# Bilinear form on one Trainium2 core: casting weight transfers of 1 MiB to 128 partitions, with a block diagonal x over four k

## The chip, the cores and the metric

The kernel runs on one core of one Trainium2 chip, with nothing on the others. The metric is the device time of one execution in microseconds (us). The kernel before was run three times.

TensorE (PE in the profile) multiplies into PSUM, with its weight loads shown apart as PEld; VectorE (DVE) does elementwise work and reductions; GpSimd (POOL) issues the transfers that change the type of what they move; SyncE (SP) and ScalarE (ACT) issue plain transfers.

## The reference

```python
def setup_inputs():
    batch, dim_i, dim_j, dim_k = 32, 256, 256, 128
    # x [32, 256], y [32, 256], weight [128, 256, 256], all float32

def reference(x, y, weight):
    return np.einsum('bi,bj,kij->bk', x, y, weight).astype(np.float32)
```

For each batch row b and each k, out[b, k] is x[b] times the 256 x 256 matrix weight[k] times y[b]. The weights are 33.55 MB in float32, and each of them is used once. Both kernels first form x[b] times weight[k] on TensorE, a row of 256 values over j, and then multiply that row by y[b] and sum over j on VectorE.

## The kernel before, in words

The weights come in by transfers from GpSimd's queue, which read float32 in HBM and write bf16 in SBUF, so 16.78 MB are written. There are 32 steps (the loop over kt), each for four k. A step's buffer, wtile, has 128 partitions in two halves of 64, and two k in each half (even k in the lower half, odd k in the upper). Each half is filled by a transfer of its own (L82): 64 partitions, two k, and per partition and k four rows of i side by side, a run of 4 KiB in HBM and of 2 KiB in SBUF. That makes 64 transfers with 128 runs each, 512 KiB read and 256 KiB written apiece. Four buffers turn (wpool, bufs=4), so the ninth transfer and each second one after it wait until TensorE has finished with the buffer of four steps ago.

TensorE makes 16 products per step (L95). Partition ip of a half holds the rows 4·ip to 4·ip+3 of i, so the sum over i takes four products (ic = 0 to 3) of 64 partitions each; the stationary operand is a 64 x 32 piece of xT, and the moving one is 64 x 256 weights of one k. Products for the lower and the upper half of the partitions alternate. The result for one k is a PSUM tile of 32 x 256, and four such tiles turn (psum, bufs=4).

VectorE takes each of these 128 results (L113): it multiplies 32 x 256 values by y and sums along j in one instruction, and a short second one writes the sum into a column of out_sb. At the end SP writes out_sb, 32 rows of 512 B (L124).

Ahead of this, x is loaded twice side by side (L53, L54), y once (L58), GpSimd makes a 32 x 32 identity (in masks.py, with the first weight transfer issued between its two steps), and TensorE transposes x in four pieces (L66), which VectorE copies to bf16 (L71).

Of the kernel before, what the change touches and what calls it, by code (L numbers as in the profile page):

```python
# [1 line left out]

# [5 lines left out]


@with_exitstack
def kernel(
    ctx: ExitStack,
    tc: tile.TileContext,
    x: bass.AP,
    y: bass.AP,
    weight: bass.AP,
    out: bass.AP,
):
    nc = tc.nc  # L20
    P = 128

    B, I = x.shape
    _, J = y.shape
    K, _, _ = weight.shape
    assert x.shape == (B, I)
    assert y.shape == (B, J)
    assert weight.shape == (K, I, J)
    assert out.shape == (B, K)

    CHUNK = 4
    HALF_P = P // 2
    assert I == HALF_P * CHUNK
    assert K <= P
    assert K % 2 == 0

    K_TILE = 4
    assert K % K_TILE == 0 and K_TILE % 2 == 0
    K_HALF = K_TILE // 2
    NUM_K_TILES = K // K_TILE  # L40
    K_SUB = max(1, min(K_HALF, 256 // J))
    assert K_HALF % K_SUB == 0

    f32 = mybir.dt.float32
    bf16 = mybir.dt.bfloat16

    consts = ctx.enter_context(tc.tile_pool(name="consts", bufs=1))
    wpool = ctx.enter_context(tc.tile_pool(name="wpool", bufs=4))
    psum_pool = ctx.enter_context(tc.tile_pool(name="psum", bufs=4, space=bass.MemoryType.PSUM))
    tmps = ctx.enter_context(tc.tile_pool(name="tmps", bufs=2))  # L50

    x2_sb = consts.tile([B, 2, I], f32)
    nc.sync.dma_start(out=x2_sb[:, 0, :], in_=x)  # L53
    nc.sync.dma_start(out=x2_sb[:, 1, :], in_=x)  # L54
    x2_flat = x2_sb.rearrange("b two i -> b (two i)")

    y_sb = consts.tile([B, J], f32)
    nc.sync.dma_start(out=y_sb, in_=y)  # L58

    identB = consts.tile([B, B], f32)  # L60
    make_identity(nc, identB)

    xT = consts.tile([P, CHUNK, B], bf16)
    for ic in range(CHUNK):
        xt_psum = psum_pool.tile([P, B], f32)
        nc.tensor.transpose(  # L66
            out=xt_psum,
            in_=x2_flat[:, ic::CHUNK],
            identity=identB,
        )  # L70
        nc.vector.tensor_copy(out=xT[:, ic, :], in_=xt_psum)  # L71

    out_sb = consts.tile([B, K], f32)

    w_rearr = weight.rearrange("k (ip ic) j -> ip k (ic j)", ic=CHUNK)

    for kt in range(NUM_K_TILES):
        k0 = kt * K_TILE

        wtile = wpool.tile([P, K_HALF, CHUNK * J], bf16)  # L80
        for kg in range(2):
            nc.gpsimd.dma_start(  # L82
                out=wtile[kg * HALF_P:(kg + 1) * HALF_P, :, :],
                in_=w_rearr[:, k0 + kg:k0 + K_TILE:2, :],
            )

        for ks in range(0, K_HALF, K_SUB):
            psums = []
            for kg in range(2):
                psum = psum_pool.tile([P, K_SUB * J], f32)  # L90
                psums.append(psum)
            for ic in range(CHUNK):
                for kg in range(2):
                    p0 = kg * HALF_P
                    nc.tensor.matmul(  # L95
                        out=psums[kg][:B, :].rearrange(
                            "b (k j) -> b k j", k=K_SUB
                        ),
                        lhsT=xT[p0:p0 + HALF_P, ic, :],
                        rhs=wtile[p0:p0 + HALF_P, ks:ks + K_SUB,  # L100
                                  ic * J:(ic + 1) * J],
                        start=(ic == 0),
                        stop=(ic == CHUNK - 1),
                    )

            for kg in range(2):
                psum_view = psums[kg][:B, :].rearrange(
                    "b (k j) -> b k j", k=K_SUB
                )
                for kk in range(K_SUB):  # L110
                    kdst = k0 + 2 * (ks + kk) + kg
                    tmp = tmps.tile([B, J], f32)
                    nc.vector.tensor_tensor_reduce(  # L113
                        out=tmp,
                        in0=psum_view[:, kk, :],
                        in1=y_sb,
                        scale=1.0,
                        scalar=0.0,
                        op0=mybir.AluOpType.mult,
                        op1=mybir.AluOpType.add,  # L120
                        accum_out=out_sb[:, kdst:kdst + 1],
                    )

    nc.sync.dma_start(out=out, in_=out_sb)  # L124


# [1 line left out]
_INS = ['x', 'y', 'weight']  # L128
_OUTS = [((32, 128), 'float32')]


# [23 lines left out]
```

## Time and profile before

| what | value |
|---|---|
| median of 3 runs | 92.71 us (92.67 to 92.99) |
| span of the profiled execution, first to last instruction | 90.9 us |
| median less span (what lies around the span) | 1.8 us |
| written by the weight queue (q0) | 16.78 MB in 9216 packets |
| HBM read | 33.65 MB |
| busy: PE, DVE, POOL | 73.9, 49.8, 38.0 us |

The profiled execution's own end-to-end time isn't given apart from its span; it is taken here as the span and the 1.8 us that the median has beyond it.

How to read it: the span is what the profiler saw between the first and the last instruction. In the table of stretches (windows), each row names a stretch in us from the span's start, its length, then the busy time of each engine in it with the number of instructions started, the granted clock of TensorE, the share in which the 16 DMA engines had a packet (it can exceed 1, since packets overlap), and the rate in GB/s, counted in bytes written. Since the weights are written in bf16, the rate of reading them is twice that. In the table of instruction groups, each row has the line, the engine, the operation, the tiles, the shape, the count, the busy time, the mean of one in ns, and the idle time of the engine ahead of them with what ended it.

### The profile page before, as it was taken

The page shows a single profiled execution, that of the slowest core. Times are in us where ns is not written, and L with a number is a line of the kernel's source. Part 1 is how long each engine was busy: PE and PEld are TensorE (multiplying, and loading weights), DVE is VectorE, ACT ScalarE, POOL GpSimd, SP SyncE. Part 2 cuts the span into 40 slices and gives each one's busy share as a digit, 9 for nine tenths or more (in the row PEclk, how much of TensorE's full clock was granted, in tenths as well). Part 3 has the DMA queues.
Part 4 walks back from the last instruction along what each step waited for, and adds up shares of the span by engine and source line. Part 5 has one row for each costly group of instructions (what it writes and reads, how often), then busy time and mean ns, then how long its engine had stood idle before and what let it go on. Part 6 is the DMA issues. An engine that isn't in the chain of part 4 may idle for free.

```text
span 90.9 us, 1569 instructions
## 1 busy us (share of the span) xinstructions
PE 73.9 (81%) x516; PEld 42.3 (47%) x516; DVE 49.8 (55%) x260; POOL 38.0 (42%) x70
## 2 busy tenths in 40 slices
PE   0248989899898989669898989898998989899970
PEld 0216444555454545435554545454555545454530
DVE  0213555676535666664556656666555565566650
POOL 5970555544435543650455554434345555500000
PEclk9999999999999999985555555555555555555555
DMA  0799999999999999999999999999999999999300
GB/s 18 121 190 186 197 208 210 207 211 213 207 208 210 208 210 209 209 209 209 211 208 212 209 209 209 211 208 215 203 210 208 211 208 212 207 210 214 53 0 7
DMA packets 9416, 16.99 MB, mean 187 GB/s; under 512 B 1088, under 2 KB 1216, under 8 KB 9408
## 3 DMA queue, kind: packets, MB, share of 16 engines
q0 software_dynamic: 9216, 16.78, 100.1%
q1 hardware_dynamic: 192, 0.11, 0.5%
q8 instruction: 4, 0.07, 0.3%
q14 instruction: 4, 0.03, 0.1%
HBM read 33.65 MB, written 0.02 MB: 370 GB/s over the span
## 4 chain that ended last, share of the span: by engine, by line
DMA 64%; PE 20%; POOL 6%; issue 6%; DVE 1%; DVEq 0%; POOLq 0%
DMA wtile<-in_weight_dram 64%; PE psum L95 20%; POOL wtile L82 6%; DVE tmp L113 1%; DVE out_sb L113 0%; POOL identB masks.py:199 0%; DVEq L150 0%; POOL identB masks.py:197 0%; POOLq masks.py:199 0%; POOLq L139 0%
## 5 line engine op out<-in xcount | busy, mean ns | idle before, releaser
L95 PE MATMUL psum<-wtile,xT 64*32 64x256 bf16 x512 | 73.2, 405 | 11.1 <-DMA wtile<-in_weight_dram 9.3
L113 DVE CUSTOM_DVE_ANT_0 tmp<-psum,y_sb 32x256 f32<-32x256 f32 x128 | 48.6, 409 | 35.4 <-PE psum L95 35.2
L95 PEld LDWEIGHTS <-xT 64*32 64x32 bf16 x512 | 41.8, 122 | 42.2 <-DMA wtile<-in_weight_dram 23.9
L82 POOL DMA_DIRECT2D wtile<-in_weight_dram x64 | 37.5, 596 | 40.7 <-PE psum L95 40.1
L113 DVE DVE_READ_ACCUMULATOR2_ANT out_sb<- 32x1 f32 x128 | 9.1, 71 | 0.0
L66 PE MATMUL xt_psum<-identB,x_sb 32*128 32x32 f32 x4 | 0.7, 300 | 3.0 <-DMA x_sb<-in_x_dram 3.0
L71 DVE CAST xT<-xt_psum 128x32 bf16<-128x32 f32 x4 | 0.6, 192 | 3.4 <-PE xt_psum L66 3.4
L66 PEld LDWEIGHTS xt_psum<-identB,x_sb 32*128 32x128 f32 x4 | 0.6, 208 | 3.0 <-POOL identB masks.py:199 3.0
masks.py:199 POOL TENSOR_SCALAR_AFFINE_SELECT identB<-identB 32x32 f32<-32x32 f32 x1 | 0.2, 229 | 0.1
masks.py:197 POOL MEMSET identB<- 32x32 f32 x1 | 0.1, 114 | 0.3 <-POOLq L139 0.3
L139 POOL MEMSET const-float32-0.0<- 128x1 f32 x1 | 0.1, 103 | 0.2 <-issue 0.2
L139 POOL MEMSET const-bfloat16-1.0<- 128x1 bf16 x1 | 0.1, 106 | 0.0
L139 POOL MEMSET const-uint8-127<- 128x1 uint8 x1 | 0.1, 106 | 0.0
L139 POOL MEMSET const-float32-1.0<- 128x1 f32 x1 | 0.1, 103 | 0.0
## 6 DMA issues: line engine op xcount, KB each, us to landing
wtile<-in_weight_dram POOLq DMA_DIRECT2D x64, 256.0 KB, 7.2
x_sb<-in_x_dram SPq DMA_DIRECT2D x2, 32.0 KB, 1.7
y_sb<-in_y_dram SPq DMA_DIRECT2D x1, 32.0 KB, 3.2
out_dram<-out_sb SPq DMA_DIRECT2D x1, 16.0 KB, 1.4
```

Source lines behind the costliest of these rows:

```text
L66: nc.tensor.transpose(out=xt_psum, in_=x2_flat[:, ic::CHUNK], identity=identB,)
L71: nc.vector.tensor_copy(out=xT[:, ic, :], in_=xt_psum)
L82: nc.gpsimd.dma_start(out=wtile[kg * HALF_P:(kg + 1) * HALF_P, :, :], in_=w_rearr[:, k0 + kg:k0 + K_TILE:2, :],)
L95: nc.tensor.matmul(out=psums[kg][:B, :].rearrange("b (k j) -> b k j", k=K_SUB), lhsT=xT[p0:p0 + HALF_P, ic, :], rhs=wtile[p0:p0 + HALF_P, ...
L113: nc.vector.tensor_tensor_reduce(out=tmp, in0=psum_view[:, kk, :], in1=y_sb, scale=1.0, scalar=0.0, op0=mybir.AluOpType.mult, op1=mybir.Al ...
L139: nc = _bacc.Bacc("TRN2", target_bir_lowering=False, num_devices=1)
```

## The change

All transfers now fill 128 partitions. The index k is split as k = 32·kk + g with kk from 0 to 3 and g from 0 to 31, and i as i = 8·ip + ic with ip from 0 to 31 and ic from 0 to 7. Partition p = 4·ip + kk holds, for one g, the eight rows ic of i for the k that belongs to kk: one run of 8 KiB in HBM and of 4 KiB in SBUF. Neighbouring partitions with the same ip are 32 k apart in HBM, which is 8 MiB. One transfer fills a step (1 MiB read, 512 KiB written, 128 runs), except the last step, which is cut into three (ic 0 to 3, 4 and 5, 6 and 7). There are 34 transfers, each with a buffer of its own, so all weights stay in SBUF as bf16 and no transfer waits for a buffer.

The stationary operand becomes block diagonal: xblk[p, ic, b, kk'] is x[b, 8·ip + ic] where kk' is the kk of the partition p, and zero elsewhere. One product of 128 partitions by 128 columns by 256 then serves 32 rows of the batch and four k at once, and its result has 128 rows (b, kk). Eight products (ic) make a step: 256 in all, in place of 512. VectorE reduces one 128 x 256 result per step, 32 in place of 128, and the output goes out as 128 rows of 128 B.

The setup changes with it: x is loaded once, y is loaded on ACT's queue to 128 partitions with each row repeated four times, the identity is 128 x 128, VectorE repeats x four times (8 copies) and makes a mask from the identity (one reduction), TensorE transposes in eight pieces, and VectorE writes xblk with four masked copies.

The diff, cut to its core (the body of the old loop and the old setup are in the listing above):

```diff
+    w_v = weight.rearrange("(kk g) (ip ic) j -> g ip kk (ic j)", kk=KK, ic=IC)
+    x_sb = consts.tile([B, I], f32)
+    nc.sync.dma_start(out=x_sb, in_=x)
+    y4 = consts.tile([P, J], f32)
+    nc.scalar.dma_start(out=y4, in_=y.unsqueeze(1).to_broadcast([B, KK, J]))
+
+    def split(g):
+        return [(0, 4), (4, 6), (6, 8)] if g == G - 1 else [(0, IC)]
+
+    def load(g):
+        for lo, hi in split(g):
+            wt = wpool.tile([P, (hi - lo) * J], bf16, name=f"w{g}_{lo}")
+            nc.gpsimd.dma_start(out=wt, in_=w_v[g][:, :, lo * J:hi * J])
...
+    load(0)
+    ident = consts.tile([P, P], f32)
+    nc.gpsimd.memset(ident, 0.0)
+    nc.gpsimd.affine_select(
...
+    for g in range(1, G):
+        load(g)
+    mask = consts.tile([P, KK], f32)
+    nc.vector.tensor_reduce(
...
+    for ic in range(IC):
+        nc.vector.tensor_copy(
+            out=x_rep[:, ic, :, :],
+            in_=x_cols[:, ic, :].unsqueeze(2).to_broadcast([B, IP, KK]),
+        )
+    xt_ps = psx.tile([P, IC, B], f32)
+    for ic in range(IC):
         nc.tensor.transpose(
...
+    xblk = consts.tile([P, IC, B, KK], bf16)
+    for kk in range(KK):
+        nc.vector.tensor_scalar(
+            out=xblk[:, :, :, kk], in0=xt_ps, scalar1=mask[:, kk:kk + 1],
+            scalar2=None, op0=mult,
+        )
...
+    for g in range(G):
+        ps = pso.tile([P, J], f32)
+        for ic in range(IC):
+            nc.tensor.matmul(
+                out=ps,
+                lhsT=xblk[:, ic, :, :].rearrange("p b kk -> p (b kk)"),
+                rhs=w_tiles[g, ic],
+                start=(ic == 0), stop=(ic == IC - 1),
+            )
+        tmp = tmps.tile([P, J], f32)
+        nc.vector.tensor_tensor_reduce(
+            out=tmp, in0=ps, in1=y4, scale=1.0, scalar=0.0,
+            op0=mult, op1=add, accum_out=acc[:, g:g + 1],
+        )
+    out_v = out.rearrange("b (kk g) -> b kk g", kk=KK)
+    nc.sync.dma_start(out=out_v, in_=acc)
```

How the instructions stand is shown for two places. The first is GpSimd's queue at the beginning of the kernel before, from the barrier that opens the program (wtile is a weight buffer, in_weight_dram the weights in HBM; the sizes are partitions, runs in a partition and elements of a run; DMASW names the completion count of an earlier weight transfer, PE that of a product).

```order
L150 UNCONDITIONAL_BRANCH [waits barrier_Pool_Activation_PE_DVE_SP_gather]
masks.py:197 MEMSET identB 32x32
L82 DMA wtile<-in_weight_dram 64x2x1024
masks.py:199 ISA
masks.py:199 AFFINE_SELECT identB<-identB 32x32 [waits Pool_49]
L82 DMA wtile<-in_weight_dram 64x2x1024 x7
L82 DMA wtile<-in_weight_dram 64x2x1024 [waits DMASW1_49,DMASW0_49,PE_49]
```

The same place in the changed kernel (w_0 stands for the weight buffers, which now have names of their own).

```order
L144 UNCONDITIONAL_BRANCH [waits barrier_Pool_Activation_PE_DVE_SP_gather]
L56 DMA w_0_74<-in_weight_dram 128x1x2048
L63 MEMSET ident 128x128
L56 DMA w_0_81<-in_weight_dram 128x1x2048
L64 ISA
L64 AFFINE_SELECT ident<-ident 128x128 [waits Pool_49]
L56 DMA w_0_83<-in_weight_dram 128x1x2048
...
L56 DMA w_0_95<-in_weight_dram 128x1x2048 [waits DMASW0_49]
```

The first weight transfer now stands ahead of the identity's memset, a second one stands ahead of the identity's last step, and the ninth transfer (w_0_95) waits for the completion of the first alone, no longer for TensorE.

The second place is TensorE's queue at the end of the kernel before: the products of the last step, with their waits for VectorE to free a PSUM tile.

```order
L95 MATMUL psum<-wtile,xT 32x256 [waits DVE_49]
L95 LDWEIGHTS xT
L95 MATMUL psum<-wtile,xT 32x256 [waits DVE_49]
L95 LDWEIGHTS xT
L95 MATMUL psum<-wtile,xT 32x256
```

The same place in the changed kernel: the last step's three pieces (w_0_141 has four products, the other two have two each).

```order
L105 LDWEIGHTS xblk [waits DMASW7_49]
L105 MATMUL ps<-w_0_141,xblk 128x256 [waits DVE_49]
...
L105 LDWEIGHTS xblk
L105 MATMUL ps<-w_4_143,xblk 128x256 [waits DMASW0_49]
...
L105 LDWEIGHTS xblk
L105 MATMUL ps<-w_6_145,xblk 128x256 [waits DMASW1_49]
L105 LDWEIGHTS xblk
L105 MATMUL ps<-w_6_145,xblk 128x256
L144 UNCONDITIONAL_BRANCH
```

What stood behind a step's last transfer were its sixteen products and four reductions; now two products stand behind the wait for the last piece, and one reduction behind those.

More of the change, by code (lines that the diff above doesn't have):

```diff
@@ L7 @@
 from concourse._compat import with_exitstack
-from concourse.masks import make_identity
 @with_exitstack
@@ L21 @@
     P = 128
+    f32 = mybir.dt.float32
+    bf16 = mybir.dt.bfloat16
+    mult = mybir.AluOpType.mult
+    add = mybir.AluOpType.add
     B, I = x.shape
@@ L25 @@
     K, _, _ = weight.shape
[L26 to L45, printed above, removed]
+    KK = P // B
@@ L47 @@
+    IP = P // KK
+    IC = I // IP
+    G = K // KK
+    assert KK * B == P and IP * KK == P and IC * IP == I and G * KK == K
     consts = ctx.enter_context(tc.tile_pool(name="consts", bufs=1))
-    wpool = ctx.enter_context(tc.tile_pool(name="wpool", bufs=4))
-    psum_pool = ctx.enter_context(tc.tile_pool(name="psum", bufs=4, space=bass.MemoryType.PSUM))
+    wpool = ctx.enter_context(tc.tile_pool(name="wpool", bufs=1))
+    psx = ctx.enter_context(tc.tile_pool(name="psx", bufs=1, space=bass.MemoryType.PSUM))
@@ L50 @@
+    pso = ctx.enter_context(tc.tile_pool(name="pso", bufs=6, space=bass.MemoryType.PSUM))
     tmps = ctx.enter_context(tc.tile_pool(name="tmps", bufs=2))
[L52 to L63, printed above, removed]
@@ L64 @@
-    for ic in range(CHUNK):
-        xt_psum = psum_pool.tile([P, B], f32)
+    w_v = weight.rearrange("(kk g) (ip ic) j -> g ip kk (ic j)", kk=KK, ic=IC)
[5 more added lines that the diff above has]
+        return [(0, 4), (4, 6), (6, 8)] if g == G - 1 else [(0, IC)]
+    w_tiles = {}
+    def load(g):
+        for lo, hi in split(g):
+            wt = wpool.tile([P, (hi - lo) * J], bf16, name=f"w{g}_{lo}")
+            nc.gpsimd.dma_start(out=wt, in_=w_v[g][:, :, lo * J:hi * J])
+            for ic in range(lo, hi):
+                w_tiles[g, ic] = wt[:, (ic - lo) * J:(ic - lo + 1) * J]
@@ new lines @@
+    load(0)
+    ident = consts.tile([P, P], f32)
+    nc.gpsimd.memset(ident, 0.0)
+    nc.gpsimd.affine_select(
+        out=ident, in_=ident, compare_op=mybir.AluOpType.not_equal, fill=1.0,
+        base=0, pattern=[[-1, P]], channel_multiplier=1,
+    )
[3 more added lines that the diff above has]
+    nc.vector.tensor_reduce(
+        out=mask, in_=ident.rearrange("p (ip kk) -> p kk ip", kk=KK),
+        axis=mybir.AxisListType.X, op=add,
+    )
+    x_rep = consts.tile([B, IC, IP, KK], f32)
@@ L66 @@
+    x_cols = x_sb.rearrange("b (ip ic) -> b ic ip", ic=IC)
+    for ic in range(IC):
[5 more added lines that the diff above has]
+    for ic in range(IC):
         nc.tensor.transpose(
-            out=xt_psum,
-            in_=x2_flat[:, ic::CHUNK],
-            identity=identB,
-        )
-        nc.vector.tensor_copy(out=xT[:, ic, :], in_=xt_psum)
@@ L73 @@
[L73 to L84, printed above, removed]
-            )
[L87 to L122, printed above, removed]
@@ L124 @@
-    nc.sync.dma_start(out=out, in_=out_sb)
+            out=xt_ps[:, ic, :],
+            in_=x_rep[:, ic, :, :].rearrange("b ip kk -> b (ip kk)"),
+            identity=ident[:B, :B],
+        )
+    xblk = consts.tile([P, IC, B, KK], bf16)
[4 more added lines that the diff above has]
+        )
+    acc = consts.tile([P, G], f32)
+    for g in range(G):
[6 more added lines that the diff above has]
+                start=(ic == 0), stop=(ic == IC - 1),
+            )
+        tmp = tmps.tile([P, J], f32)
+        nc.vector.tensor_tensor_reduce(
+            out=tmp, in0=ps, in1=y4, scale=1.0, scalar=0.0,
+            op0=mult, op1=add, accum_out=acc[:, g:g + 1],
+        )
```

## The prediction

> **What bounds the kernel now.** I read the page first: the slices, the queues, the chain that ended last.
>
> ```profile
> span 90.9 us, 1569 instructions
> DMA  0799999999999999999999999999999999999300
> DMA packets 9416, 16.99 MB, mean 187 GB/s; under 512 B 1088, under 2 KB 1216, under 8 KB 9408
> q0 software_dynamic: 9216, 16.78, 100.1%
> DMA 64%; PE 20%; POOL 6%; issue 6%; DVE 1%; DVEq 0%; POOLq 0%
> ```
>
> The DMA engines are busy from the second slice to the third from last, and the chain leads through them for 64% of the span. PE is busy for 81% of it, so I looked at what it waits for, in the groups by line.
>
> ```profile
> L95 PE MATMUL psum<-wtile,xT 64*32 64x256 bf16 x512 | 73.2, 405 | 11.1 <-DMA wtile<-in_weight_dram 9.3
> L113 DVE CUSTOM_DVE_ANT_0 tmp<-psum,y_sb 32x256 f32<-32x256 f32 x128 | 48.6, 409 | 35.4 <-PE psum L95 35.2
> L113 DVE DVE_READ_ACCUMULATOR2_ANT out_sb<- 32x1 f32 x128 | 9.1, 71 | 0.0
> L82 POOL DMA_DIRECT2D wtile<-in_weight_dram x64 | 37.5, 596 | 40.7 <-PE psum L95 40.1
> ```
>
> TensorE waits for weights, VectorE for TensorE, and GpSimd for TensorE to free a buffer. GpSimd's 40.1 us of waiting would matter if the queue ran empty. The stretches say that it doesn't (stretch, length, then PE, PEld, DVE, POOL, the clock, the DMA share, GB/s written):
>
> ```profile
> 1.00:10.00 9.00, 4.29 (x27) 2.55 (x29) 2.54 (x14) 5.67 (x11) 1.00 0.88 148
> 10.00:84.00 74.00, 65.81 (x468) 37.74 (x466) 44.53 (x234) 32.00 (x55) 0.70 1.12 210
> 84.00:86.00 2.00, 1.89 (x15) 1.04 (x11) 1.10 (x5) 0.00 (x0) 0.50 0.40 71
> ```
>
> For 74 us the rate is 210 GB/s written, 420 read. Together: 9 x 148 + 74 x 210 + 2 x 71 = 17,014 KB, the page's 16.99 MB. So the time is a start, a stream at 210, and a tail. The start and the end of the stream:
>
> ```profile
> 3.20:3.40 0.20, 0.20 (x4) 0.20 (x3) 0.03 (x1) 0.20 (x1) 1.00 0.17 20
> 3.40:3.60 0.20, 0.20 (x3) 0.16 (x2) 0.20 (x2) 0.20 (x2) 1.00 0.93 113
> 3.60:3.80 0.20, 0.09 (x1) 0.10 (x1) 0.20 (x3) 0.20 (x1) 1.00 0.87 184
> 5.00:10.00 5.00, 3.64 (x23) 1.91 (x24) 1.99 (x10) 2.03 (x5) 1.00 1.11 185
> 85.40:85.60 0.20, 0.20 (x4) 0.01 (x1) 0.20 (x1) 0.00 (x0) 0.50 0.17 31
> 85.60:85.80 0.20, 0.20 (x2) 0.00 (x0) 0.20 (x3) 0.00 (x0) 0.50 0.01 0
> ```
>
> Weights flow from about 3.4 us, at the full rate after a ramp that loses 0.2. From 5 to 10 us the rate is 185, which costs 5 x 25 / 210 = 0.6 us, for a reason that I don't see. About 0.13 MB other than weights (instructions above all; 0.21 MB less what moved before 3.4) take 0.5. So 3.4 + 0.2 + 16.78 MB / 210 (79.9) + 0.6 + 0.5 = 84.6, where the stream would end at the full rate; since the engines finish apart, the last data come at 85.6, 0.9 to 1.0 later.
>
> **The change part by part.** *The stream.* The same 16.78 MB are written, and the rate decides. The queue's 9216 packets are 64 x 144: on each of 16 engines a transfer is 8 data packets and one more small one (1024 of the page's 1088 under 512 B). A transfer takes 262 KB / 210 = 1.248 us. After, 8 data packets carry twice the bytes. Lower bound of a gain: if time goes by bytes alone, 210 stays. Upper bound: if each of the 9 packets costs a fixed 1.248 / 9 = 139 ns for its present size, and only the small packet's share is halved, 512 KiB take 8 x 277 + 139 = 2.36 us, 222 GB/s. The share of 1.12 says that packets overlap on an engine and hide much of what is fixed, so I stay near the low end: 213.5, that is 78.6 us, 1.3 less than now.
>
> The Trainium skill, "DMA: Bandwidth & Descriptors", section "Bandwidth", prices a packet's fixed overhead at about 3 cycles of 32 B; by that, an estimate, 4 KiB reads cost 131 cycles and 8 KiB reads 259, a gain of 1.2% or some 0.9 us (the rate would be 212.5), and its ceiling of 435 GB/s read is 217.6 written, 77.1 us. No row before the change separates the fixed part from the bytes.
>
> *The start.* GpSimd issues the first weight transfer ahead of the memset, not behind it.
>
> ```profile
> 0.74 0.11 POOL masks.py:197 MEMSET identB<- 32x32 f32 x1 [0.29 <-POOLq L139]
> 1.28 0.72 POOL L82 DMA_DIRECT2D wtile<-in_weight_dram  x1 [0.42 <-issue]
> 2.24 4.10 POOL L82 DMA_DIRECT2D wtile<-in_weight_dram  x7
> ```
>
> The memset's 0.11 us is the gain; data come 2.1 us after the issue (1.28 to 3.4), so from 3.3. Each issue takes 0.6 us of GpSimd for the same 128 runs but now feeds 2.45 us of transfers, so the second one may stand behind a memset, and the ramp of 0.2 us shrinks to 0.1. Of the dips of 0.6 us I keep 0.3 (bounds 0 and 0.6). Other data: 0.4 in place of 0.5, with half of TensorE's instructions to fetch. The larger y moves while the first weights are being issued.
>
> *Setup behind that.* x lands 1.7 us after its issue and its first transfer suffices. Eight copies, eight transposes in their cover, a reduction and four masked copies follow. Nearest rows: the old casts and transposes, and L113 for 256 elements on VectorE.
>
> ```profile
> L66 PE MATMUL xt_psum<-identB,x_sb 32*128 32x32 f32 x4 | 0.7, 300 | 3.0 <-DMA x_sb<-in_x_dram 3.0
> L71 DVE CAST xT<-xt_psum 128x32 bf16<-128x32 f32 x4 | 0.6, 192 | 3.4 <-PE xt_psum L66 3.4
> x_sb<-in_x_dram SPq DMA_DIRECT2D x2, 32.0 KB, 1.7
> ```
>
> 8 x 0.19 + 0.41 + 0.3 + 4 x 0.41 = 3.9 us from about 2.5, so xblk stands at 6.4 (at 0.41 for each copy too, 8.1). The first step lands at about 3.3 + 2.45 + 0.4 = 6.2. At worst TensorE starts 1.9 us late, with 75 us to catch up, and no transfer waits for it any more. Cost nothing; the stream covers it.
>
> *The products.* A step now brings eight of 128 partitions and 128 columns, in 2.45 us: 306 ns for each.
>
> ```profile
> 40.92 2.29 PE L95 MATMUL psum<-wtile,xT 64*32 64x256 bf16 x16 [0.60 <-DMA wtile<-in_weight_dram]
> 38.48 1.04 PE L95 MATMUL psum<-wtile,xT 64*32 64x256 bf16 x12 [0.71 <-DVE out_sb L113]
> L95 PE MATMUL psum<-wtile,xT 64*32 64x256 bf16 x22 | 2.4, 271 | 0.9 <-DVE out_sb L113 0.7 <-DMA wtile<-in_weight_dram 0.2
> L95 PE MATMUL psum<-wtile,xT 64*32 64x256 bf16 x98 | 14.7, 411 | 2.0 <-DMA wtile<-in_weight_dram 1.7 <-DVE out_sb L113 0.2
> L95 PE MATMUL psum<-wtile,xT 64*32 64x256 bf16 x102 | 14.7, 412 | 1.4 <-DMA wtile<-in_weight_dram 1.4
> L95 PEld LDWEIGHTS <-xT 64*32 64x32 bf16 x512 | 41.8, 122 | 42.2 <-DMA wtile<-in_weight_dram 23.9
> ```
>
> The rows with x22, x98 and x102 are the groups of three stretches: 37.3 to 40.2, 20 to 36, and 60 to 76 us. Sixteen take 2.29 us with the last one's 0.41: (2.29 - 0.41) / 15 = 125 ns apart, and since two halves of the partitions alternate, 250 ns within a half. That is the row for a product of 256 columns. Shorter is possible: the twelve at 38.48, of 0.27 each, stand (1.04 - 0.27) / 11 = 70 apart, 140 within a half. Longer: if all of the 122 ns of a weight load came on top, 372. I take 250, 2.0 us per step, and TensorE waits for the stream. VectorE has 32 x 0.48 us in place of 128.
>
> *The tail.* Before, the last step shows this:
>
> ```profile
> 83.61 1.69 PE psum L95 x8
> 86.10 1.69 PE psum L95 x8
> 88.57 0.01 DVE out_sb L113
> 88.61 0.33 SPq L124 DMA_DIRECT2D out_dram<-out_sb  x1
> out_dram<-out_sb SPq DMA_DIRECT2D x1, 16.0 KB, 1.4
> y_sb<-in_y_dram SPq DMA_DIRECT2D x1, 32.0 KB, 3.2
> ```
>
> From 86.10 it takes 2.48 us to VectorE's end at 88.58, and 2.3 from there to the end of the span, 4.8 in all. After: two products (0.25 + 0.41), one reduction with its short second part (0.03 + 0.41 + 0.07), 1.2 us; then 2.3, and for 128 rows of 128 B in place of 32 of 512 B I add 0.2 (bounds: 0, and 1.5, since y landed in 3.2 us where x took 1.7). 3.7 in all.
>
> *The sum.* 3.3 + 0.1 + 78.6 + 0.3 + 0.4 = 82.7; 0.9 for engines that finish apart, 83.6; 0.4 from the last data to the first product, 84.0 (before: 85.6 to 86.1, partly the queue of results); tail 3.7: a span of 87.7 in place of 90.9. With the 1.8 us that the median has beyond the span: 89.5 us.
>
> **The rivals.** *The rate stays at 210.* Time goes by bytes, or a run of 8 KiB is moved as two. The stream takes 79.9, the time is 90.8. For it: 210 hardly moves over 74 us. Against it: the small packets that go. The change would then not do to the rate what its larger runs stand for.
>
> *The rate rises to the upper bound.* At 217 to 222 GB/s the stream takes 77.3 to 75.6, and the time is 88.2 to 86.5. Single rows of 1 us reach that, none lasts:
>
> ```profile
> 22.00:23.00 1.00, 0.77 (x9) 0.43 (x9) 0.70 (x6) 0.94 (x2) 1.00 1.12 219
> 23.00:24.00 1.00, 1.00 (x8) 0.58 (x5) 0.42 (x2) 0.23 (x1) 1.00 1.12 203
> ```
>
> *Slower: reads that lie 8 MiB apart disturb each other.* Before, a transfer reads two k that are 512 KiB apart; after, neighbouring partitions read 8 MiB apart, four deep. Of the 3.2 us that the sum gains, 1.9 lie outside the stream, so the change turns slower once the stream takes more than 79.9 + 1.9 = 81.8 us, below 205 GB/s. At the 185 of the row from 5 to 10 us it would take 90.7, and the time would be 101.6 us. Against it: partitions of the same kk read only 8 KiB apart, so the reads of one transfer spread over four blocks of 256 KiB, each without gaps. The Trainium skill, "DMA: Bandwidth & Descriptors", section "Latency and other measured facts", has plain copies with a row pitch of 8 MiB at half the rate of those with 512 KiB; no row before the change has such a pitch.
>
> *TensorE becomes the bound.* From 306 ns per product on. The row's 250 is for 32 columns of weights and 256 moving ones; if time goes by their sum, 384 in place of 288, a product takes 333 ns, a step 2.67, and 32 of them 85.3 from 6.4 on, 91.7; with 0.5 + 2.3 + 1.8 that is 96.3 us, and at 372 it is 106.2. Against it: the twelve products at 38.48 ran at 140, so a faster pace is there, and it came after a stretch with little waiting. "TensorE: Matmul & The Clock Gate" of the Trainium skill, section "LDWEIGHTS (loading the stationary operand)", has a weight load go by its columns, 107 ns for 128 of them where 32 take 27: an estimate of 330 by it. The granted clock can't decide: it reads 1.00 before 40 us and 0.50 after, for products of the same length (411 and 412 ns in the stretches on either side).
>
> **How the numbers follow.** My forecast (88.9 to 90.2) gets 0.46, the rate at 210 (up to 91.4) 0.26, the higher rate 0.16, the pitch 0.07, TensorE 0.05. Against no change, about 0.5% can be told by a measurement of this kernel. Faster by more than that: 0.46 + 0.26 + 0.16, less 0.02 for a tail at its upper bound behind a rate of 210 (92.1 and a little more), 0.86. Same: these 0.02 and 0.01 of TensorE, where it finds its faster pace part of the way, 0.03. Slower: the pitch and the rest of TensorE, 0.11. The range takes in forecast and steady rate, and of the higher rate what lies down to 217: 88.0 to 91.5.
>
> **What would show it.** Right: 212 to 215 GB/s from 10 us to the end, weights flowing from 3.3 us, PE waiting for weights, the last reduction 1.2 us behind the last landing. Wrong: a rate below 205 with TensorE waiting (the pitch); TensorE without idle time ahead of its products and a product spacing above 306 ns (TensorE); an output that lands later than 2 us after its issue (the tail).

## The result and the profile after

The changed kernel takes 88.97 us (median of 4 runs, 88.65 to 89.71), the kernel before beside it 92.69 us (91.93 to 92.99): a ratio of 0.9622, with a 95% interval of 0.9563 to 0.9681. The prediction was 89.5 us in a range of 88.0 to 91.5. The profiled execution is the slowest of the four: 89.71 us, of which 87.9 are the span.

The page of the changed kernel, the same parts as before (span, DMA slices, packets, the weight queue, the chain, then two groups):

```profile
span 87.9 us, 727 instructions
DMA  0999999999999999999999999999999999999600
DMA packets 5235, 17.00 MB, mean 193 GB/s; under 512 B 720, under 2 KB 1136, under 8 KB 5232
q0 software_dynamic: 4896, 16.78, 96.3%
DMA 86%; POOL 4%; PE 4%; issue 2%; DVE 0%; POOLq 0%; DVEq 0%
L105 PE MATMUL ps<-w,xblk 128*128 128x256 bf16 x256 | 51.7, 372 | 29.3 <-DMA w<-in_weight_dram 29.3
L56 POOL DMA_DIRECT2D w<-in_weight_dram x34 | 18.2, 542 | 50.8 <-DMA w<-in_weight_dram 50.0
```

The kernel is bound by the stream more plainly than before: 86% of the chain. TensorE waits 29.3 us, and for weights alone. GpSimd waits for earlier transfers, not for TensorE.

For the stretches I cut at 12 us, where the start is over in both kernels. Before:

```profile
1.00:12.00 11.00, 6.29 (x40) 3.73 (x40) 3.48 (x19) 6.15 (x12) 1.00 0.93 159
12.00:80.00 68.00, 60.24 (x429) 34.69 (x430) 40.77 (x213) 31.51 (x54) 0.71 1.12 209
```

After, and below it the weights' first data and a hole in the rate behind them:

```profile
1.00:12.00 11.00, 4.87 (x25) 3.39 (x26) 4.90 (x17) 5.99 (x12) 1.00 0.93 180
12.00:80.00 68.00, 43.70 (x223) 25.86 (x223) 11.69 (x54) 12.66 (x24) 0.69 1.06 213
3.00:3.20 0.20, 0.11 (x1) 0.11 (x2) 0.20 (x3) 0.20 (x2) 1.00 0.00 0
3.20:3.40 0.20, 0.20 (x3) 0.20 (x4) 0.20 (x3) 0.20 (x1) 1.00 0.81 164
3.80:4.00 0.20, 0.20 (x4) 0.20 (x2) 0.16 (x1) 0.20 (x1) 1.00 0.28 20
```

By 12 us the changed kernel has moved 11 x 180 = 1980 KB against 11 x 159 = 1750. These 230 KB aren't all weights, since y now goes to 128 partitions. The queues of x, y and the output, one before and two after (q10 is y's):

```profile
q1 hardware_dynamic: 192, 0.11, 0.5%
q10 hardware_dynamic: 144, 0.13, 0.5%
q1 hardware_dynamic: 192, 0.05, 0.3%
```

They moved 0.07 MB more than before, and y lands at about 3.2 us (2.5 us behind its issue at 0.74), ahead of the weights. The weight queue alone moved 1.65 MB from 1 to 12 us before and 1.81 MB after: 0.16 MB, which at 213 GB/s is 0.75 us. From there on 213 GB/s against 209 make 15.0 MB shorter by 1.3 to 1.4 us. The last data:

```profile
83.40:83.60 0.20, 0.20 (x3) 0.15 (x1) 0.16 (x1) 0.00 (x0) 0.50 0.10 15
83.60:83.80 0.20, 0.20 (x3) 0.15 (x1) 0.20 (x2) 0.00 (x0) 0.50 0.01 0
```

They come at 83.5 us (85.6 before). The end of the chain in order of time:

```profile
61.81 0.28 issue
62.09 19.38 DMA w<-in_weight_dram
81.47 0.05 issue
81.51 3.61 PE ps L105 x16
85.12 0.02 issue
85.15 0.42 DVE tmp L112
```

It is not the last landing from which this execution ends, but the landing of the whole step 30 at 81.47: sixteen products, of step 30 and of step 31, follow without a gap for 3.61 us. So the 3.0 us between the two spans are about 0.75 of start and 1.35 of stream, together the 2.1 us by which the last data come earlier (85.6 less 83.5), and 0.9 of tail: 5.3 us lie behind the last data before, 4.4 after.

### The profile page after: what moved, and what is told of

The parts are those of the page before. It is cut to its first block, busy times and chain, and to the rows that moved or that the text cites. A ratio compares the mean times of both kernels' runs of the same rounds, so it can differ in the third digit from the quotient of the medians.

```text
span 87.9 us, 727 instructions
## 1 busy us (share of the span) xinstructions
PE 52.7 (60%) x264; PEld 31.6 (36%) x264; DVE 17.9 (20%) x77; POOL 18.9 (21%) x40
## 4 chain that ended last, share of the span: by engine, by line
DMA 86%; POOL 4%; PE 4%; issue 2%; DVE 0%; POOLq 0%; DVEq 0%
DMA w<-in_weight_dram 86%; PE ps L105 4%; POOL w L56 3%; DVE tmp L112 0%; POOL ident L64 0%; POOL ident L63 0%; POOLq L64 0%; POOLq L133 0%; DVEq L144 0%
## 5 line engine op out<-in xcount | busy, mean ns | idle before, releaser
L105 PE MATMUL ps<-w,xblk 128*128 128x256 bf16 x256 | 51.7, 372 | 29.3 <-DMA w<-in_weight_dram 29.3
L105 PEld LDWEIGHTS <-xblk 128*128 128x128 bf16 x256 | 30.7, 128 | 50.0 <-DMA w<-in_weight_dram 32.1
L56 POOL DMA_DIRECT2D w<-in_weight_dram x34 | 18.2, 542 | 50.8 <-DMA w<-in_weight_dram 50.0
L112 DVE CUSTOM_DVE_ANT_0 tmp<-ps,y 128x256 f32<-128x256 f32 x32 | 13.6, 425 | 65.1 <-PE ps L105 65.1
L87 PE MATMUL xt_ps<-ident,x_rep 32*128 32x32 f32 x8 | 1.1, 292 | 3.1 <-POOL ident L64 3.1
L112 DVE DVE_READ_ACCUMULATOR2_ANT acc<- 128x1 f32 x32 | 2.7, 83 | 0.0
L96 DVE TENSOR_SCALAR xblk<-xt_ps,mask 128x256 bf16<-128x256 f32 x4 | 2.5, 772 | 0.2 <-PE xt_ps L87 0.2
L87 PEld LDWEIGHTS xt_ps<-ident,x_rep 32*128 32x128 f32 x8 | 0.9, 215 | 3.1 <-POOL ident L64 3.1
L81 DVE COPY x_rep<-x_sb 32x128 f32<-32x128 f32 x8 | 1.3, 228 | 2.4 <-DMA x_sb<-in_x_dram 2.4
```

The costliest lines, as they stand in the source:

```text
L56: nc.gpsimd.dma_start(out=wt, in_=w_v[g][:, :, lo * J:hi * J])
L81: nc.vector.tensor_copy(out=x_rep[:, ic, :, :], in_=x_cols[:, ic, :].unsqueeze(2).to_broadcast([B, IP, KK]),)
L87: nc.tensor.transpose(out=xt_ps[:, ic, :], in_=x_rep[:, ic, :, :].rearrange("b ip kk -> b (ip kk)"), identity=ident[:B, :B],)
L96: nc.vector.tensor_scalar(out=xblk[:, :, :, kk], in0=xt_ps, scalar1=mask[:, kk:kk + 1], scalar2=None, op0=mult,)
L105: nc.tensor.matmul(out=ps, lhsT=xblk[:, ic, :, :].rearrange("p b kk -> p (b kk)"), rhs=w_tiles[g, ic], start=(ic == 0), stop=(ic == IC - 1),)
L112: nc.vector.tensor_tensor_reduce(out=tmp, in0=ps, in1=y4, scale=1.0, scalar=0.0, op0=mult, op1=add, accum_out=acc[:, g:g + 1],)
```

## The experiments

**Does the longer run make the rate?** Two edits with runs of 4 KiB. The first (e1) splits each load:

```diff
-        return [(0, 4), (4, 6), (6, 8)] if g == G - 1 else [(0, IC)]
+        return [(0, 4), (4, 6), (6, 8)] if g == G - 1 else [(0, 4), (4, 8)]
```

> The changed kernel with each step loaded by two transfers (ic 0 to 3, ic 4 to 7): 128 partitions and no waits on TensorE as in the changed kernel, but runs of 4 KiB and 65 transfers of 512 KiB read. Theory runs (a fixed cost per data packet, so longer runs made 213 GB/s of 210): 210 GB/s between 10 and 80 us, time 90.1 us (1.15 more than 88.97). Theory small packets (the completion packets, one per transfer and engine): also 210, 90.1. Theory partitions (128 of them in a transfer, in place of two halves of 64): 213, 89.0. Theory waits (transfers that no longer wait for TensorE): 213, 89.0.

Measured: 91.33 us (91.31 to 91.6), ratio 0.9843 (0.9788 to 0.9898). The rate is read finer from the chain, where GpSimd's waits stand exactly eight transfers apart. The kernel before, then this one:

```profile
60.93 0.04 issue
60.97 1.90 PE psum L95 x14
...
70.95 0.04 issue
```

```profile
75.08 0.28 issue
75.36 9.74 DMA w<-in_weight_dram
85.10 0.05 issue
```

10.02 us per eight transfers of 512 KiB in both (70.95 - 60.93, and 85.10 - 75.08). So neither the 128 partitions nor the waits that went make the rate; theories partitions and waits fall. In each of these chains one wait is longer: 11.03 us before (19.83 to 30.86), 10.75 here (34.19 to 44.94), and 20.45 in the changed kernel (21.70 to 42.15), where eight transfers otherwise take 19.66. In each of the three an instruction fetch of 16 KiB (queue q8), which took 0.9 us on one engine, falls into that wait, at 22, 34 and 32 us. That it makes the landing late is likely but wasn't tested, and later fetches in these traces show no such wait. I compare stretches without a late landing; the other waits of the two kernels lie between 10.01 and 10.11 us.

By 12 us it had moved 11 x 160 = 1760 KB, and of weights 1.60 MB, no more than the 1.65 before the change: the start's gain went with the runs as well.

```profile
1.00:12.00 11.00, 5.12 (x27) 3.44 (x28) 5.02 (x17) 7.05 (x15) 1.00 0.91 160
```

The second (e2) keeps the runs at 4 KiB and makes the transfers 1 MiB:

```diff
+    w_p = weight.rearrange("(gp g2 kk) (ip ic) j -> gp (kk ip) g2 (ic j)", kk=KK, g2=2, ic=IC)
...
+            for lo, hi in [(0, 4), (4, 8)]:
+                wt = wpool.tile([P, 2, (hi - lo) * J], bf16, name=f"w{g}_{lo}")
+                nc.gpsimd.dma_start(out=wt, in_=w_p[g // 2][:, :, lo * J:hi * J])
...
```

> Runs of 4 KiB with transfers of 1 MiB read: 128 partitions, two steps and half of the ic in one transfer, 256 runs, 34 transfers. The weights are taken with k = 4g + kk and partition = 32 kk + ip, and x and the output columns are not rearranged to match, so the output isn't the reference's; the work is the same. Theory runs: 210 GB/s, 90.1 us. Theory small packets: 213, 89.0. Theories partitions and waits: 213, 89.0.

Measured: 93.86 us, but four runs lie between 91.66 and 94.26, so no verdict rests on its time. The profile is of the 91.66.

```profile
49.16 0.29 issue
49.45 19.60 DMA w<-in_weight_dram
69.04 0.28 issue
```

Eight transfers of 1 MiB in 19.88 us, 211.0 GB/s: between the two theories. Both count, the length of the runs and the number of transfers. Its start is the worst of all, 148 GB/s in the stretch to 12 us (11 x 148 = 1630 KB, 1.46 MB of them weights).

**Halves at 8 KiB.** Halves of 64 partitions are tried by themselves, with the long runs kept (e15):

```diff
-            nc.gpsimd.dma_start(out=wt, in_=w_v[g][:, :, lo * J:hi * J])
+            for h in range(2):
+                nc.gpsimd.dma_start(
+                    out=wt[h * 64:(h + 1) * 64, :],
+                    in_=w_v[g][h * 16:(h + 1) * 16, :, lo * J:hi * J],
+                )
```

> The changed kernel with each load done by two transfers, one for the lower and one for the upper 64 partitions, as before the change; runs of 8 KiB, 64 runs and 512 KiB to a transfer, 68 transfers. If the runs alone make the rate: 213 GB/s, 8 transfers in 9.83 us, 89.0 us. If the number of transfers counts too, as between the two runs with 4 KiB (10.02 us per 8 of 512 KiB, 19.88 per 8 of 1 MiB; 20 ns for a transfer's end by these two): 8 x (4 x 304.7 + 20) = 9.91 us, 211.6, 89.6 us. If halves of 64 partitions cost something of their own: 209 or less as before the change, 90.5 us or more.

Measured: 90.17 us (90.03 to 90.58), ratio 0.9753 (0.9690 to 0.9817). The chain:

```profile
62.18 0.28 issue
62.46 9.62 DMA w<-in_weight_dram
72.08 0.28 issue
```

72.08 - 62.18 = 9.90 us (9.91 in most of the other waits), where the number of transfers and the length of the runs alone give 9.91. Halves cost nothing in the stream beyond the transfers that they add. The time is 0.6 us above that expectation; the stretch to 12 us holds a part of it (177 GB/s against 180, 0.15 us), and the rest is open.

**Where the gain of longer runs ends.** Runs of 16 KiB, then two runs of 8 KiB to a partition, both in transfers of 2 MiB:

```diff
+    w_p = weight.rearrange("(kk gp) (ip ic) j -> gp ip kk (ic j)", kk=2 * KK, ic=2 * IC)
...
+            wt = wpool.tile([P, 2 * IC * J], bf16, name=f"w{g}_0")
+            nc.gpsimd.dma_start(out=wt, in_=w_p[g // 2])
...
```

> Runs of 16 KiB (sixteen rows of i), 2 MiB read per transfer, 128 runs, except the last two steps, which are loaded as in the changed kernel. The products use the same stationary operand for both halves of a run, so the output isn't the reference's; their number is the same. Theory runs: the fixed cost halves once more, 214.5 to 215 GB/s, 88.3 us. Theory small packets: 215, 88.3. Theories partitions and waits: 213, 89.0. If something else than packets sets the limit at 8 KiB already (a run moved in pieces): 213, 89.0.

TensorE starts on a transfer as soon as it has landed, so its starts are the landings:

```profile
38.81 1.92 PE L115 MATMUL ps<-w,xblk 128*128 128x256 bf16 x16 [0.77 <-DMA w<-in_weight_dram]
73.17 1.92 PE L115 MATMUL ps<-w,xblk 128*128 128x256 bf16 x16 [1.41 <-DMA w<-in_weight_dram]
78.24 5.39 PE L115 MATMUL ps<-w,xblk 128*128 128x256 bf16 x32 [3.15 <-DMA w<-in_weight_dram]
```

88.42 us (88.26 to 88.83), ratio 0.9529 (0.9472 to 0.9587), so the time is near the 88.3 of two theories, but not by their way. Eight transfers take 39.43 us, 212.7 GB/s. The last of them lands a little late, and the seven up to 73.17 take 34.36 us, 4.909 each: 213.6, where the theories have 214.5 and more. The gain lies in the start, 193 GB/s to 12 us, 2120 KB (1.96 MB of weights):

```profile
1.00:12.00 11.00, 4.33 (x24) 3.31 (x25) 4.51 (x15) 5.23 (x11) 1.00 0.94 193
```

```diff
+    w_p = weight.rearrange("(gp g2 kk) (ip ic) j -> gp (kk ip) g2 (ic j)", kk=KK, g2=2, ic=IC)
...
+            wt = wpool.tile([P, 2, IC * J], bf16, name=f"w{g}_0")
+            nc.gpsimd.dma_start(out=wt, in_=w_p[g // 2])
...
```

> Runs of 8 KiB, two to a partition: transfers of 2 MiB read in blocks of 1 MiB (k = 4g + kk, partition = 32 kk + ip; x and the output columns are not rearranged to match, so the output isn't the reference's). Theory of two fixed costs, from three runs so far (4 KiB read at 10.02 us per 8 transfers of 512 KiB, 19.88 per 8 of 1 MiB with 256 runs, 8 KiB read at 19.66 per 8 of 1 MiB with 128): a 4 KiB read takes 154 ns on its engine, an 8 KiB read 304.7, a transfer's end 20 ns. By it 8 transfers of 2 MiB take 8 x (16 x 304.7 + 20) = 39.16 us, 214.2 GB/s, 0.4% more than the changed kernel, 0.3 us over the stream. Rival: 8 KiB reads are at a limit of 213.3, as 16 KiB reads were at 212.7 (39.43 us): 39.3 to 39.4 us. On the start: transfers of 256 runs lost more of it in the run with 4 KiB, so the stream is late by 1 us and the time 89.5 to 90 us; if runs of 8 KiB cure the start, 88.7.

TensorE's starts again, and the instruction queue in the stretch from 72 to 73 us:

```profile
39.62 1.92 PE L115 MATMUL ps<-w,xblk 128*128 128x256 bf16 x16 [1.03 <-DMA w<-in_weight_dram]
68.95 3.51 PE L115 MATMUL ps<-w,xblk 128*128 128x256 bf16 x16 [2.95 <-DMA w<-in_weight_dram]
74.59 2.60 PE L115 MATMUL ps<-w,xblk 128*128 128x256 bf16 x16 [2.12 <-DMA w<-in_weight_dram]
78.92 5.39 PE L115 MATMUL ps<-w,xblk 128*128 128x256 bf16 x32 [1.73 <-DMA w<-in_weight_dram]
q8 instruction: 1, 0.02, 6.1%
```

Eight transfers take 39.3 us by these rows (39.31 between the waits in the chain, 213.4 GB/s), and that looks like the rival's limit. But the landing at 74.59 is late: it comes 5.64 us after the one before it, just behind an instruction fetch of 16 KiB that held an engine for 1 us. The six transfers from 39.62 to 68.95 take 29.33 us, 4.888 each, 214.5 GB/s, where the theory of two fixed costs has 4.895. So the theory holds for transfers of 2 MiB too, the rate goes beyond the rival's limit of 213.3, and at this size of transfer runs of 16 KiB (4.909) are no faster than runs of 8 KiB. The time is 89.26 us (88.94 to 89.57), no less than the changed kernel's: the start has lost again, 1.75 MB of weights by 12 us against 1.81.

**The pitch of 8 MiB.**

```diff
-    w_v = weight.rearrange("(kk g) (ip ic) j -> g ip kk (ic j)", kk=KK, ic=IC)
+    w_v = weight.rearrange("(g kk) (ip ic) j -> g (kk ip) (ic j)", kk=KK, ic=IC)
...
```

> The changed kernel with transfers that read 1 MiB in one block (k = 4g + kk, partition = 32 kk + ip) in place of four blocks 8 MiB apart; x and the output columns are not rearranged to match, so the output isn't the reference's. Theory: a pitch of 8 MiB costs nothing here, 213 GB/s, 89.0 us. Rival: the pitch costs some of what longer runs gain, so without it 215 or more, 88.2 us or less.

89.13 us (88.72 to 89.5), ratio 0.9584 (0.9509 to 0.9659), and its chain:

```profile
61.58 0.28 issue
61.86 19.38 DMA w<-in_weight_dram
81.25 0.05 issue
```

81.25 - 61.58 = 19.67 us, and 81.47 - 61.81 = 19.66 in the changed kernel. The pitch costs nothing here, and the rival that turned on it falls.

**The start.** Three edits: no setup on VectorE and TensorE, four loads ahead of the identity, and GpSimd paced to three queued transfers.

```diff
-    mask = consts.tile([P, KK], f32)
...
+    xblk = consts.tile([P, IC, B, KK], bf16)
+    nc.vector.memset(xblk, 0.5)
```

> The changed kernel without VectorE's and TensorE's setup: x_rep, the mask, the transposes and the masked copies are left out, and xblk is filled with one constant, so the output isn't the reference's. Theory: VectorE's setup from 2.4 to 6.7 us slows the issue of the first transfers, and with it the stream, which moves 1978 KB by 12 us; without it the dip from 3 to 5 us goes and 2080 to 2100 KB have moved by 12 us, 88.5 us. Rival: the dip is the stream's own (the first reads, or GpSimd's eight issues in a row): 1978 KB as before, 89.0 us.

89.0 us (88.85 to 89.46), and 11 x 183 = 2010 KB by 12 us. The other runs with the start of the changed kernel have 180 to 185 there, so the rival holds: VectorE's setup isn't the cause.

```diff
-    load(0)
+    for g in range(4):
+        load(g)
...
```

> The changed kernel with four weight transfers ahead of the identity (in place of one), so that the second is issued some 0.15 us earlier and the setup on VectorE and TensorE begins about 1.3 us later. Theory: the order of these issues is free, since the first transfer has 2.4 us of work in it: the start moves by less than 0.1 us and TensorE catches up, 89.0 us. Rival: engines without a second transfer queued at 2.6 us idle, so an earlier second issue gains 0.2 to 0.3 us, 88.7.

89.26 us (89.01 to 89.72), ratio 0.9628 (0.9588 to 0.9668), with 187 GB/s to 12 us, against 180 to 185 in the others: 0.1 to 0.4 us of start, none of it in the time. For the time the theory (the order is free) holds.

```diff
...
     for g in range(1, G):
+        if g >= 3:
+            nc.gpsimd.tensor_copy(out=pace, in_=w_tiles[g - 3, 0][:, 0:1])
         load(g)
```

> The changed kernel with GpSimd paced from the fourth transfer on: before it issues the load of step g it copies one column of step g-3's buffer, so that it waits for that one's landing, and no more than three transfers are queued. Theory: eight transfers issued in a row (1.2 to 6.2 us) slow the engines' start, since the dip in the rate was the longer the more runs were issued meanwhile; with three issued by 3.5 us the rate is full from about 3.5 us, 2080 KB or more are moved by 12 us (1979 to 2029 in the runs with eight), and the time falls by 0.3 to 0.5 us, 88.5. Rival: the start is slow whatever is queued: 1980 to 2030 KB, 89.0 us. Second rival: three queued transfers are too few for engines that run apart, the rate in the stream falls below 213, 89.5 us or more.

90.98 us (89.53 to 92.0), ratio 0.9729 (0.9668 to 0.9790). The profiled execution took 91.95 us.

```profile
1.00:12.00 11.00, 4.85 (x25) 3.36 (x26) 4.90 (x17) 3.55 (x9) 1.00 0.91 181
12.00:80.00 68.00, 44.27 (x216) 26.05 (x215) 11.25 (x52) 19.80 (x56) 0.66 1.05 208
```

The start is as slow with three transfers queued (181) as with eight, so my theory of the eight issues falls. The second rival fits: 208 GB/s in this stream, and six runs that lie 2.5 us apart. Since this is one of the longest of the six, it isn't shown that the rate fell in the others, of which the three shortest took 89.53, 90.34 and 90.87. What makes the start slow is open: it goes with the length of the runs (159 and 160 GB/s to 12 us with 4 KiB, 177 to 187 with 8 KiB, 193 with 16 KiB), and two runs to a partition make it slower (148 with 4 KiB, 174 with 8). No other edit moved it by more than 0.4 us.

**The tail.** Three edits of it: the last two steps in pieces, the last step whole, and a TensorE kept busy by products into a spare tile.

```diff
-        return [(0, 4), (4, 6), (6, 8)] if g == G - 1 else [(0, IC)]
+        return [(0, 2), (2, 4), (4, 6), (6, 8)] if g >= G - 2 else [(0, IC)]
```

> The changed kernel with the last two steps both loaded in four pieces (two ic each). Theory: the end is set by TensorE from the landing of the whole step 30 (81.47 us) on, sixteen products at 212 ns; with pieces it can begin earlier, and the end is the last piece's landing and two products: 0.4 to 0.6 us less, 88.5 us. Rival: the last landing is the limit (late engines), and eight small pieces make it 0.2 us later: 89.0 to 89.2 us.

```diff
-        return [(0, 4), (4, 6), (6, 8)] if g == G - 1 else [(0, IC)]
+        return [(0, IC)]
```

> The changed kernel with the last step loaded by one transfer in place of three pieces. Theory: eight products stand behind the last landing in place of two, 0.67 us more at the fast pace (8 products 1.05 us, 2 products 0.38) and up to 1.3 more at the slow one (1.89 against 0.6), less 0.1 to 0.2 for two transfers and the short runs that go: 89.5 to 90.1 us. Rival: the pieces' landings are late anyway (the engines that finish last decide) and the split is worth nothing: 88.9 to 89.1.

```diff
...
+        if g < G - 2:
+            for ic in range(IC):
+                nc.tensor.matmul(
+                    out=spare,
+                    lhsT=xblk[:, ic, :, :].rearrange("p b kk -> p (b kk)"),
+                    rhs=w_tiles[g, ic],
+                    start=True, stop=True,
+                )
```

> The changed kernel with eight more products per step, up to step 29, into a spare PSUM tile that nothing reads, so that TensorE is busy most of the time. Theory: TensorE's granted clock stays near full, the last sixteen products are 111 ns apart rather than 212, and the end moves from 85.1 to the last landing plus some, 0.6 to 1.0 us less: 88.2 us. Rival 1: the last landing (84.2 or later) is the limit and the faster clock brings 0.3 us or less. Rival 2: the clock falls all the same before the end, or the extra products at the slow clock (3.4 us a step, against 2.46 of the stream) leave TensorE behind: 89.5 us or more.

TensorE's last products in these three (pieces, last step whole, kept busy), from their timelines:

```profile
83.85 0.38 PE L105 MATMUL ps<-w,xblk 128*128 128x256 bf16 x2 [0.27 <-DMA w<-in_weight_dram]
```

```profile
83.48 1.77 PE L105 MATMUL ps<-w,xblk 128*128 128x256 bf16 x8 [0.59 <-DMA w<-in_weight_dram]
```

```profile
81.39 1.05 PE L106 MATMUL ps<-w,xblk 128*128 128x256 bf16 x8 [0.58 <-DMA w<-in_weight_dram]
...
83.89 0.38 PE L106 MATMUL ps<-w,xblk 128*128 128x256 bf16 x2 [0.28 <-DMA w<-in_weight_dram]
```

With pieces, and with a fast TensorE, two products stand behind the last landing, at 83.85 and 83.89: the last landing is the limit, at about 83.9. The times are 89.19 (88.99 to 89.46) and 89.03 us (88.52 to 89.49), no better than the changed kernel's 88.97, so the rival holds in the one and rival 1 in the other. The granted clock was 1.00 throughout with the added products (0.72 in the changed kernel). In the profiled changed kernel VectorE ended at 85.58 and in these at 84.7: 0.8 to 0.9 us, about what the slow clock cost this execution at its end. Whether it makes the 1.1 us between the changed kernel's four runs isn't shown: only one of them has a trace, and the six with the added products, at granted clocks of 0.99 to 1.00, lie 1.0 us apart as well (88.52 to 89.49). With the last step whole, eight products follow its landing, and the time is 89.98 us (89.5 to 90.17), ratio 0.9692 (0.9652 to 0.9733): the split into pieces is worth about 1.0 us, as its theory had it.

## Why the prediction was right, point by point

*The stream: 213.5 GB/s, 1.3 us less.* Right: 19.66 us per eight transfers are 213.3, and 1.35 us. The prediction took a point between 210 and 222 by judgment, without knowing how the small costs divide, so that it came within 0.2 GB/s is luck. Four runs now say how they divide. Per 1 MiB read an engine has 16 packets of 4 KiB and two transfers' ends in 10.02 / 4 = 2.505 us (e1), 16 and one in 2.485 (e2), 8 of 8 KiB and two ends in 9.91 / 4 = 2.4775 (e15), 8 and one in 2.4575 (the change). Either pair gives 20 ns for a transfer's end; since the waits are read to 0.01 us and repeat to some hundredths, that is good to a few ns. A packet of 4 KiB then takes 154.1 ns and one of 8 KiB 304.7: 150.6 ns for 4 KiB of data and 3.5 ns for the packet itself. Over all 32 MiB (the 1.35 us above are for the part after 12 us) the longer runs save 32 x (16 x 154.1 - 8 x 304.7) = 0.9 us and the halved number of transfers 32 x 20 ns = 0.6 us. The upper bound of 222, a packet's full price for each transfer's end, was far off.

The Trainium skill's page "DMA: Bandwidth & Descriptors", section "Bandwidth", has an overhead of about 3 cycles per packet, and 32 B and 850 MHz for each of 16 ports; an estimate from these, with the 3 cycles taken at 850 MHz too, is 3.5 ns for the packet and 150.6 ns for 4 KiB of data. The page has the 32 B for the ports to SBUF; counted in bytes read, as the prediction counted its 435 GB/s, these runs agree with both, transfers of 2 MiB with 8 KiB runs too. With runs of 16 KiB they don't: by the same figures, again an estimate, a packet of 16 KiB would take 4 x 150.6 + 3.5 = 605.9 ns and a transfer of 2 MiB 8 x 605.9 + 20 ns = 4.867 us, and it took 4.909.

*The start: 3.3 us, then 0.4 lost.* Right in the place (first data in the row 3.20 to 3.40) and about right in the sum: 3.3 + 0.4 gives (12 - 3.7) x 213.5 = 1770 KB of weights by 12 us, against 1810. The reasons were not: I let the ramp shrink because each issue feeds more, and kept half of the dip for caution. With halves at 8 KiB an issue feeds half as much, and 1.78 MB of weights had come by 12 us; with transfers of the same 512 KiB and runs of 4 KiB it was 1.60, with the kernel before 1.65. So the gain goes with the length of the runs and hardly with what an issue feeds. It is 0.75 us, about half of what the rate brings, and the prediction had counted 0.5 for it (0.1 for the first data, 0.1 for the ramp, 0.3 for the dip). Its 0.13 MB of other data are 0.6 us at 210 GB/s, not 0.5; the forecast doesn't hang on this.

*The setup.* xblk was forecast at 6.4 us and stood at 6.7, and TensorE's first product came at 6.95, when the first step had landed (forecast: 6.2). The setup's parts were off both ways: the eight copies took 1.25 us in all where I had 1.5, the masked copies, priced at 0.41 each, took 0.77:

```profile
L96 DVE TENSOR_SCALAR xblk<-xt_ps,mask 128x256 bf16<-128x256 f32 x4 | 2.5, 772 | 0.2 <-PE xt_ps L87 0.2
```

As forecast it cost nothing: without all of it the time was 89.0.

*The products: 250 ns, no bound.* The last sixteen, where the granted clock reads 0.50:

```profile
81.51 3.59 PE L105 MATMUL ps<-w,xblk 128*128 128x256 bf16 x16 [0.93 <-DMA w<-in_weight_dram]
```

With 0.41 us for the last one they stand (3.59 - 0.41) / 15 = 212 ns apart; at full clock two took 0.38 and eight 1.05, six more in 0.67, 111 ns each. So 250 was too much, and nothing hung on it. Weights of 128 columns cost no more than those of 32, and the rival in which the time goes by the sum of the columns (333 ns) falls.

*The tail: 3.7 us from 84.0.* The mechanism, two products behind the last landing, is what the runs with pieces and with a busy TensorE show, from 83.9. In the profiled execution it failed: TensorE at its slow clock had sixteen products to do from 81.47 on and ended 85.1, about 0.6 us later than two slow products behind a landing at 83.9 would have. The sign that the prediction named, a last reduction 1.2 us behind the last landing, isn't there: it ended 2.1 us behind the last data (0.9 behind the landing in the two runs). I had checked that TensorE keeps up on average (2.0 us a step against 2.45) and not that the last step's pieces land within one step of their forerunner. VectorE's end at 85.58 was 0.4 later than forecast, and the output, 128 rows of 128 B, landed in 1.5 us where I allowed 1.6.

*The sum.* A span of 87.7 was forecast, 87.9 measured in the profiled execution, and 86.9 to 87.9 over the four. That the profiled one comes within 0.2 us is partly luck: its last data came at 83.5 where 83.6 was forecast, and its tail took 4.4 us where 0.4 + 3.7 = 4.1 was.

*The rivals.* The rate at 210 and the higher one were ruled out by 213.3, the pitch by the run without it, TensorE as the bound by its 29.3 us of waiting, except for the last two steps.

## What to carry to other kernels

A transfer that is limited by its engines has a small price per packet and one per transfer; they can be had to a few nanoseconds from two runs that differ in one of them, if the stretches compared have no late landing. Such prices have a range: here they still held for transfers of 2 MiB with runs of 8 KiB (214.5 GB/s written), and no more for runs of 16 KiB (213.6). Count the start of a stream as a term of its own: in this kernel the first 12 us were worth 0.75 us, about half as much as 2% of rate, and bytes other than the stream's must be taken off before two starts are compared. At the end look at what lands together: an engine that keeps up on average can still have two steps' work behind one landing.

## What the runs showed that I had not expected

The queue's depth counts even where the DMA slices are nearly all at 9: with three transfers of 1 MiB queued six runs took 89.53 to 92.0 us (208 GB/s in the profiled one), with eight queued four took 88.65 to 89.71 (213). TensorE's granted clock reads 1.00 at the start of a trace and can't be believed there: in the changed kernel eight products took 1.86 us at 6.95, where it reads 1.00, and 1.89 at 24.18, where it reads 0.50. With products added to keep TensorE busy the last products were fast and the clock read 1.00 to the end, and the kernel was no faster. The kernel with runs of 16 KiB was the fastest of all (88.42 us), by its start and not by its rate; its transfers bring eight k at once, for which one stationary operand of 128 columns doesn't do, so a kernel with the reference's output would need twice the products. That one was not tried.
